# Rotary embedding on half the head, f32: interleaving batches on partitions so that one shuffle spreads the tables

## The chip, the cores and the metric

One core of a Trainium2 chip. (The sets of runs below came from different chips; each set has the kernel before beside it.) The metric is the device time of one execution in microseconds (us). A time is a median over runs; runs of one kernel mostly agree within 0.3%, and all runs quoted here are fast (granted clock 1.00). Profiles give a span that is about 1.8 us shorter than the measured time of the same run.

## The reference

```
x: (16, 512, 16, 64) f32    cos, sin: (512, 32) f32
x1, x2 = x[..., :32], x[..., 32:]
first  = x1[..., :16] * cos[..., :16] - x1[..., 16:] * sin[..., :16]
second = x1[..., :16] * sin[..., :16] + x1[..., 16:] * cos[..., :16]
out = concatenate([first, second, x2])
```

x is 33.55 MB and out is 33.55 MB. Half of every head is only copied, so the kernel moves 67.1 MB and computes on half of what it loads. The tables depend on the sequence position alone, not on the batch.

## The kernel before

x is seen as 512 runs of 16 sequence positions, 64 KB each. A tile is 128 consecutive runs, one per partition, and there are four tiles and a ring of three buffers. A batch has 32 runs, so partition p needs table row p mod 32: the 32 rows are loaded onto partitions 0 to 31 and copied four times.

```
    xf = x.rearrange("b s h d -> (b s h d)").rearrange("(t p f) -> t p f", t=T, p=P)
    of = out.rearrange("b s h d -> (b s h d)").rearrange("(t p f) -> t p f", t=T, p=P)
    ...
    ring = const_pool.tile([P, NS, K, H, D], fp32)          # NS = 3, K = 16
    stage = const_pool.tile([PB, 2, K, HF], fp32)           # PB = 32
    table = const_pool.tile([P, 2, K, 2, Q], fp32)
    ...
    nc.gpsimd.dma_start(out=stage[:, 0]..., in_=cosf)
    nc.gpsimd.dma_start(out=stage[:, 1]..., in_=sinf)
    load(0, 0, K0); load(0, K0, K); load(1); load(2, 0, KC)  # K0 = 4, KC = 8, on nc.sync
    for r in range(REP):                                     # REP = 4
        nc.vector.tensor_copy(out=table[r * PB : (r + 1) * PB]..., in_=stage...)
    ...                     # rotate: two multiplies, a subtract, an add on VectorE
    rotate(0, 0, K0); rotate(0, K0, (K0 + K) // 2); rotate(0, (K0 + K) // 2, K)
    store(0); load(2, KC, K); load(3)
    for t in range(1, T):
        rotate(t, 0, KC); rotate(t, KC, K); store(t)
```

All loads of x and all stores go through one queue (q1 on the page, 67.11 MB), and they follow each other in the order of issue: tile 0, tile 1, half of tile 2, store 0, the other half of tile 2, tile 3, and the stores of tiles 1, 2 and 3.

Of the kernel before, what the change touches and what calls it, by code (L numbers as in the profile page):

```python
# [1 line left out]

# [4 lines left out]


@with_exitstack
def kernel(  # L10
    ctx: ExitStack,
    tc: tile.TileContext,
    x: bass.AP,
    cos: bass.AP,
    sin: bass.AP,
    out: bass.AP,
):
    nc = tc.nc
    fp32 = mybir.dt.float32
    P = 128  # L20
    B, S, H, D = x.shape
    Q = D // 4
    HF = D // 2



    K = 16
    T = B * S // (P * K)
    PB = S // K
    REP = P // PB  # L30
    R = H * D
    NS = 3
    KC = K // 2
    K0 = K // 4

    xf = x.rearrange("b s h d -> (b s h d)").rearrange("(t p f) -> t p f", t=T, p=P)
    of = out.rearrange("b s h d -> (b s h d)").rearrange("(t p f) -> t p f", t=T, p=P)
    cosf = cos.rearrange("(p k) j -> p (k j)", k=K)
    sinf = sin.rearrange("(p k) j -> p (k j)", k=K)

    const_pool = ctx.enter_context(tc.tile_pool(name="const", bufs=1))
    b_pool = ctx.enter_context(tc.tile_pool(name="bp", bufs=1, space=bass.MemoryType.PSUM))


    ring = const_pool.tile([P, NS, K, H, D], fp32)
    stage = const_pool.tile([PB, 2, K, HF], fp32)
    table = const_pool.tile([P, 2, K, 2, Q], fp32)

    def rows(t, lo, hi):
        return ring[:, t % NS, lo:hi].rearrange("p k h d -> p (k h d)")  # L50

    def load(t, lo=0, hi=K):
        nc.sync.dma_start(out=rows(t, lo, hi), in_=xf[t, :, lo * R : hi * R])  # L53

    def store(t, lo=0, hi=K):
        nc.sync.dma_start(out=of[t, :, lo * R : hi * R], in_=rows(t, lo, hi))

    nc.gpsimd.dma_start(out=stage[:, 0].rearrange("p k j -> p (k j)"), in_=cosf)  # L58
    nc.gpsimd.dma_start(out=stage[:, 1].rearrange("p k j -> p (k j)"), in_=sinf)  # L59
    load(0, 0, K0)  # L60
    load(0, K0, K)
    load(1)
    load(2, 0, KC)


    for r in range(REP):
        nc.vector.tensor_copy(  # L67
            out=table[r * PB : (r + 1) * PB].rearrange("p t k c j -> p (t k) c j"),
            in_=stage.rearrange("p t k j -> p (t k) j")[:, :, 0:Q]
            .unsqueeze(2)  # L70
            .to_broadcast((PB, 2 * K, 2, Q)),
        )
    C = table[:, 0].rearrange("p k c j -> p k (c j)")
    Sn = table[:, 1].rearrange("p k c j -> p k (c j)")

    def rotate(t, lo, hi):
        n = hi - lo
        x1 = ring[:, t % NS, lo:hi, :, 0:HF]
        c = C[:, lo:hi].unsqueeze(2).to_broadcast((P, n, H, HF))
        s = Sn[:, lo:hi].unsqueeze(2).to_broadcast((P, n, H, HF))  # L80
        b_full = b_pool.tile([P, KC, H, HF], fp32, name="b_t")
        b_t = b_full[:, 0:n]
        nc.vector.tensor_mul(out=b_t, in0=x1, in1=s)  # L83
        nc.vector.tensor_mul(out=x1, in0=x1, in1=c)  # L84
        nc.vector.tensor_sub(  # L85
            out=x1[:, :, :, 0:Q], in0=x1[:, :, :, 0:Q], in1=b_t[:, :, :, Q:HF]
        )
        nc.vector.tensor_add(  # L88
            out=x1[:, :, :, Q:HF], in0=x1[:, :, :, Q:HF], in1=b_t[:, :, :, 0:Q]
        )  # L90

    rotate(0, 0, K0)
    rotate(0, K0, (K0 + K) // 2)
    rotate(0, (K0 + K) // 2, K)
    store(0)
    load(2, KC, K)
    load(3)
    for t in range(1, T):
        rotate(t, 0, KC)
        rotate(t, KC, K)  # L100
        store(t)


# [1 line left out]
_INS = ['x', 'cos', 'sin']  # L105
_OUTS = [((16, 512, 16, 64), 'float32')]


# [23 lines left out]
```

## Time and profile before

| | before |
|---|---|
| time, median | 161.8 us |
| span of the profile | 160.1 us |
| DMA queue of x and out, share of 16 engines | 97.8% |
| VectorE busy | 110.0 us (69%) |
| first multiply starts | 11.94 us |

The DMA queue lines of the page (queue, kind: packets, MB, share of the time of 16 engines):

```profile
q1 hardware_dynamic: 1440, 67.11, 97.8%
q0 software_dynamic: 64, 0.13, 0.2%
```

The table by stage (stretch in us, its length, busy us and instructions of VectorE and GpSimd, clock, DMA share, GB/s):

```profile
10.00:50.00 40.00, 34.92 (x17) 0.00 (x0) 1.00 1.00 434
50.00:100.00 50.00, 47.55 (x15) 0.00 (x0) 1.00 1.00 430
100.00:156.00 56.00, 26.68 (x8) 0.00 (x0) 1.00 1.02 440
```

The kernel is bound by its transfers: from 10 to 156 us the 16 engines are busy all the time (DMA share 1.00 to 1.02) at 430 to 440 GB/s. VectorE, busy for 69% of the span, has slack.

The start of the timeline (start us, us, engine, line, operation; in brackets the idle time before and what ended it; DVE is VectorE, POOL is GpSimd, SPq is SyncE, which issues the transfers of x and out):

```profile
0.74 1.88 SPq L53 DMA_DIRECT2D ring<-in_x_dram  x4
1.25 0.63 POOL L58 DMA_DIRECT2D stage<-in_cos_dram  x1 [0.81 <-PEq L127]
...
9.13 2.77 DVE L67 COPY table<-stage 32x1024 f32<-32x1024 f32 x4 [9.13 <-DMA stage<-in_sin_dram]
11.94 2.30 DVE L83 TENSOR_TENSOR b_t<-ring,table 128x2048 f32<-128x2048 f32 x1
...
23.66 3.37 DVE L83 TENSOR_TENSOR b_t<-ring,table 128x3072 f32<-128x3072 f32 x1 [4.71 <-DMA ring<-in_x_dram]
```

The chain of waits, its transfers only (start us, us, what):

```profile
0.74 0.38 SPq L53
...
1.17 22.39 DMA ring<-in_x_dram
...
44.14 28.18 DMA out_dram<-ring
72.34 28.75 DMA ring<-in_x_dram
```

The ends of these pieces are landings: the rest of tile 0 landed at 23.56 us, store 0 at 72.32 us, tile 3 at 101.09 us.

### The profile page before, as it was taken

Reading aid. Unit: us, or ns where it says so; the run is one execution under the profiler, and the core shown is the slowest. Engines: PE = TensorE matmul, PEld = TensorE weight load, DVE = VectorE, ACT = ScalarE, POOL = GpSimd, SP = SyncE. Lnnn points to the kernel's source line nnn. Section 1 sums busy time; section 2 is a strip of 40 time slices with the busy share of each in tenths; the row PEclk is TensorE's granted clock in tenths of the full one; section 3 lists DMA queues with packets and bytes.
Section 4 is the critical chain, followed back from the end, with each engine's and each line's share of the span. In section 5 each row is a group of like instructions: output and inputs, shape, how many; then the busy total and the mean of one; then the engine's idle time right before and its main releaser. Section 6 shows DMA issues by size and latency. Waiting matters only on the chain.

```text
span 160.1 us, 109 instructions
## 1 busy us (share of the span) xinstructions
DVE 110.0 (69%) x40; POOL 1.3 (1%) x6
## 2 busy tenths in 40 slices
DVE  0069709999999999999999994799999900000000
POOL 3000000000000000000000000000000000000000
DMA  6999999699699799899996996996996996996991
GB/s 197 385 504 454 393 459 524 262 524 491 295 401 581 328 524 409 377 393 418 483 540 295 491 524 262 524 524 262 524 524 262 524 524 262 524 491 295 524 459 66
DMA packets 1504, 67.24 MB, mean 420 GB/s; under 512 B 192, under 2 KB 192, under 8 KB 224
## 3 DMA queue, kind: packets, MB, share of 16 engines
q1 hardware_dynamic: 1440, 67.11, 97.8%
q0 software_dynamic: 64, 0.13, 0.2%
HBM read 33.69 MB, written 33.55 MB: 420 GB/s over the span
## 4 chain that ended last, share of the span: by engine, by line
DMA 50%; DVE 28%; DVEq 1%; issue 0%; SPq 0%
DMA ring<-in_x_dram 32%; DMA out_dram<-ring 18%; DVE b_t L83 10%; DVE ring L84 10%; DVE ring L85 5%; DVE ring L88 3%; DVEq L127 1%; SPq L53 0%; DVEq L83 0%
## 5 line engine op out<-in xcount | busy, mean ns | idle before, releaser
L83 DVE TENSOR_TENSOR b_t<-ring,table 128x4096 f32<-128x4096 f32 (+2 forms) x9 | 35.6, 3959 | 8.2 <-DMA ring<-in_x_dram 8.0
L84 DVE TENSOR_TENSOR ring<-ring,table 128x4096 f32<-128x4096 f32 (+2 forms) x9 | 35.6, 3950 | 0.3
L85 DVE TENSOR_TENSOR ring<-ring,b_t 128x2048 f32<-128x2048 f32 (+2 forms) x9 | 18.4, 2049 | 0.3
L88 DVE TENSOR_TENSOR ring<-ring,b_t 128x2048 f32<-128x2048 f32 (+2 forms) x9 | 18.4, 2042 | 0.0
L67 DVE COPY table<-stage 32x1024 f32<-32x1024 f32 x4 | 2.7, 684 | 9.2 <-DMA stage<-in_sin_dram 9.1
L58 POOL DMA_DIRECT2D stage<-in_cos_dram x1 | 0.6, 631 | 0.8 <-PEq L127 0.8
L59 POOL DMA_DIRECT2D stage<-in_sin_dram x1 | 0.5, 498 | 0.0
L116 POOL MEMSET const-bfloat16-1.0<- 128x1 bf16 x1 | 0.1, 102 | 0.0
L116 POOL MEMSET const-float32-0.0<- 128x1 f32 x1 | 0.1, 99 | 0.2 <-issue 0.2
L116 POOL MEMSET const-float32-1.0<- 128x1 f32 x1 | 0.1, 99 | 0.0
L116 POOL MEMSET const-uint8-127<- 128x1 uint8 x1 | 0.1, 99 | 0.0
## 6 DMA issues: line engine op xcount, KB each, us to landing
ring<-in_x_dram SPq DMA_DIRECT2D x2, 4096.0 KB, 43.9
ring<-in_x_dram SPq DMA_DIRECT2D x1, 6144.0 KB, 22.4
ring<-in_x_dram SPq DMA_DIRECT2D x1, 2048.0 KB, 8.5
stage<-in_cos_dram POOLq DMA_DIRECT2D x1, 64.0 KB, 6.0
stage<-in_sin_dram POOLq DMA_DIRECT2D x1, 64.0 KB, 7.2
out_dram<-ring SPq DMA_DIRECT2D x4, 36.4
ring<-in_x_dram SPq DMA_DIRECT2D x2, 35.0
```

The source lines that it names most:

```text
L58: nc.gpsimd.dma_start(out=stage[:, 0].rearrange("p k j -> p (k j)"), in_=cosf)
L59: nc.gpsimd.dma_start(out=stage[:, 1].rearrange("p k j -> p (k j)"), in_=sinf)
L67: nc.vector.tensor_copy(out=table[r * PB : (r + 1) * PB].rearrange("p t k c j -> p (t k) c j"), in_=stage.rearrange("p t k j -> p (t k) j" ...
L83: nc.vector.tensor_mul(out=b_t, in0=x1, in1=s)
L84: nc.vector.tensor_mul(out=x1, in0=x1, in1=c)
L85: nc.vector.tensor_sub(out=x1[:, :, :, 0:Q], in0=x1[:, :, :, 0:Q], in1=b_t[:, :, :, Q:HF])
L88: nc.vector.tensor_add(out=x1[:, :, :, Q:HF], in0=x1[:, :, :, Q:HF], in1=b_t[:, :, :, 0:Q])
L116: nc = _bacc.Bacc("TRN2", target_bir_lowering=False, num_devices=1)
L127: with _tile.TileContext(nc) as tc:
```

## The change

The intent is to spread the tables by one VectorE instruction for all 128 partitions instead of four for 32. The shuffle of the edit is given one mask with 32 entries, p // 4 * 4, for the 128 partitions, and the four partitions that need one table row are made neighbours: partition 4j+b takes run j of batch b, the table rows land on every fourth partition, and one shuffle copies each to the next three. The part of the stage that is read is first set to zero on all 128 partitions, and the table loads wait for that.

```diff
-    xf = x.rearrange("b s h d -> (b s h d)").rearrange("(t p f) -> t p f", t=T, p=P)
-    of = out.rearrange("b s h d -> (b s h d)").rearrange("(t p f) -> t p f", t=T, p=P)
+    xf = x.rearrange("(t b) (j k) h d -> t j b (k h d)", t=T, k=K)
+    of = out.rearrange("(t b) (j k) h d -> t j b (k h d)", t=T, k=K)
 ...
-    stage = const_pool.tile([PB, 2, K, HF], fp32)
+    stage = const_pool.tile([P, 2, K, HF], fp32)
 ...
-    nc.gpsimd.dma_start(out=stage[:, 0].rearrange("p k j -> p (k j)"), in_=cosf)
-    nc.gpsimd.dma_start(out=stage[:, 1].rearrange("p k j -> p (k j)"), in_=sinf)
+    nc.vector.memset(stage[:, :, :, 0:Q], 0.0)
+    first = stage.rearrange("(j b) t k i -> j b t (k i)", b=REP)
+    nc.gpsimd.dma_start(out=first[:, 0, 0], in_=cosf)
+    nc.gpsimd.dma_start(out=first[:, 0, 1], in_=sinf)
 ...
-    for r in range(REP):
-        nc.vector.tensor_copy(...)
+    nc.vector.stream_shuffle(out=table..., in_=stage...,
+        mask=[p // REP * REP for p in range(32)])
```

The transfers of x and out now have three dimensions on the HBM side (32 runs, 4 batches 2 MB apart, the row) instead of two.

More of the change, by code (lines that the diff above doesn't have):

```diff
@@ L52, in load @@
     def load(t, lo=0, hi=K):
-        nc.sync.dma_start(out=rows(t, lo, hi), in_=xf[t, :, lo * R : hi * R])
+        nc.sync.dma_start(out=rows(t, lo, hi), in_=xf[t, :, :, lo * R : hi * R])
     def store(t, lo=0, hi=K):
-        nc.sync.dma_start(out=of[t, :, lo * R : hi * R], in_=rows(t, lo, hi))
-    nc.gpsimd.dma_start(out=stage[:, 0].rearrange("p k j -> p (k j)"), in_=cosf)
-    nc.gpsimd.dma_start(out=stage[:, 1].rearrange("p k j -> p (k j)"), in_=sinf)
+        nc.sync.dma_start(out=of[t, :, :, lo * R : hi * R], in_=rows(t, lo, hi))
+    nc.vector.memset(stage[:, :, :, 0:Q], 0.0)
+    first = stage.rearrange("(j b) t k i -> j b t (k i)", b=REP)
+    nc.gpsimd.dma_start(out=first[:, 0, 0], in_=cosf)
+    nc.gpsimd.dma_start(out=first[:, 0, 1], in_=sinf)
     load(0, 0, K0)
@@ L63 @@
     load(2, 0, KC)
-    for r in range(REP):
-        nc.vector.tensor_copy(
-            out=table[r * PB : (r + 1) * PB].rearrange("p t k c j -> p (t k) c j"),
-            in_=stage.rearrange("p t k j -> p (t k) j")[:, :, 0:Q]
-            .unsqueeze(2)
-            .to_broadcast((PB, 2 * K, 2, Q)),
-        )
+    nc.vector.stream_shuffle(
+        out=table.rearrange("p t k c j -> p (t k) c j"),
+        in_=stage.rearrange("p t k j -> p (t k) j")[:, :, 0:Q]
+        .unsqueeze(2)
+        .to_broadcast((P, 2 * K, 2, Q)),
+        mask=[p // REP * REP for p in range(32)],
+    )
     C = table[:, 0].rearrange("p k c j -> p k (c j)")
```

## The prediction

> **What bounds it now.** The 16 DMA engines. The page's queue line gives the x/out queue 97.8% of 16 engines' span, and a table by stage reads 434, 430 and 440 GB/s in 10-50, 50-100 and 100-156 us, at a DMA share of 1.00 to 1.02: every engine always has a packet.[...] 67.11 MB at 434 GB/s is 154.6 us; about 2 us of start, 1 us lost in 2-10 us (373 GB/s) and 3 us of end complete the span of 160.1. VectorE is busy for 110.0 us (69%) and idles 32 us at the end.
>
> **What the change does.**
> 1. Table spread: four 32x1024 copies (684 ns each, 2.77 us in the timeline) become one 128x1024 shuffle.[...] Estimate 1.2-1.4 us, saving about 1.4.
> 2. Added: a 128x512 memset, an estimated 0.4-0.7 us, and the table loads (issued at 1.25 us) now wait for it: about 0.5 us later. Table rows also land on every fourth partition[...]. I expect landing at 9.5-11.5 us instead of 9.1; the first multiply starts between 11 and 13 us (11.94 before). Nearly a wash.
> 3. Moved: partition 4j+b takes run j of batch b. Bytes, row lengths (16 to 64 KB) and transfers stay; four neighbouring partitions are now 2 MB apart in HBM instead of adjacent, and the HBM side has one more dimension. Packets should still be one per row, on all 16 engines. Issue may get slower (four loads take 1.88 us now), perhaps by 0.1-0.3 us each; only the first counts.
>
> **On the critical path.** Almost nothing. VectorE ends the first quarter tile at 18.95 us and then waits 4.71 us for the second load, so a table earlier or later by up to 4.7 us changes no store. Even that load isn't binding: the store of tile 0 is issued at 44.1 us while about 20 MB of loads keep the engines busy to about 50 us. The chain of waits puts 28% on VectorE, but the saturated stages show that work to be covered. So I expect 0 to +0.3 us from a later first transfer, and no gain from the shuffle.
>
> **Predicted time**: 161.9 us; 161.4 to 163.0 should hold it 8 times in 10. Faster by over 2%: 0.01; within 2%: 0.94; slower by over 2%: 0.05.
>
> **What would show the steps right.** One shuffle of 1.1-1.5 us in the groups view; the wait for the table ends at 9.5-11.5 us; the wait before the second multiply takes up what the table stage lost or won; it ends at 23.3-24.3 us; main-stage rate 430-440 GB/s; 1440 packets on the x/out queue; VectorE busy about 109 us.
>
> **What would make it wrong.** (a) HBM disliking the new order[...]. [...]I don't expect it; it would show as a rate below 425 GB/s. (b) Transfers divided over fewer or unevenly loaded engines[...]; the DMA share would fall[...]. (c) A table landing later than about 16 us. (d) A start later by more than 0.3 us.

Passages of the recorded text that rested on rules not shown by any trace of this case are cut; the places are marked. The forecast's sum is the 161.8 us measured before plus 0 to 0.3 us for a later first transfer, which came to 161.9 us. The 0.4 to 0.7 us for the memset and the 0.1 to 0.3 us for a slower issue are estimates, with no derivation.

## The result, and the profile after

The changed kernel took 163.44 us median (162.95 to 164.49, 6 runs) against 161.80 us (161.75 to 162.16, 6 runs): a ratio of 1.0101, 95% interval 1.0068 to 1.0134. (Ratios divide the mean time of one kernel's fast runs by that of the other's of the same rounds, so they are not quite the ratio of the medians.) It is clearly slower by about 1%, 163.44 us where 161.9 were predicted. The outputs are right.

DMA queue lines of the page, after:

```profile
q1 hardware_dynamic: 1440, 67.11, 97.3%
q0 software_dynamic: 64, 0.13, 0.2%
```

The table by stage, after:

```profile
10.00:50.00 40.00, 33.58 (x15) 0.00 (x0) 1.00 1.00 427
50.00:100.00 50.00, 47.28 (x15) 0.00 (x0) 1.00 1.01 430
100.00:156.00 56.00, 26.68 (x8) 0.00 (x0) 1.00 0.99 431
```

These stages count a packet's bytes where it starts, and 16 packets of 64 KB are 1 MB, so differences of some GB/s over 50 us are not meaningful. They show no general slowdown.

The start of the timeline, after:

```profile
0.73 2.65 SPq L54 DMA_DIRECT2D ring<-in_x_dram  x4
0.92 0.48 DVE L59 MEMSET stage<- 128x512 f32 x1 [0.92 <-PEq L120]
1.71 0.65 POOL L61 DMA_DIRECT2D stage<-in_cos_dram  x1 [1.26 <-DVE stage L59]
...
8.95 0.01 DVE L70 LOAD_MASK_SELECT table<-stage  x1 [7.55 <-DMA stage<-in_sin_dram]
8.98 1.29 DVE L70 STREAM_SHUFFLE table<-stage 128x1024 f32<-128x1024 f32 x1
10.30 2.30 DVE L87 TENSOR_TENSOR b_t<-ring,table 128x2048 f32<-128x2048 f32 x1
...
23.39 3.37 DVE L87 TENSOR_TENSOR b_t<-ring,table 128x3072 f32<-128x3072 f32 x1 [6.08 <-DMA ring<-in_x_dram]
```

VectorE did what was intended. The shuffle took 1.29 us instead of the 2.77 of the four copies, and the first multiply starts 1.64 us earlier. The four first issues take 2.65 us instead of 1.88.

The chain of waits, its transfers only, after:

```profile
0.73 0.67 SPq L54
...
1.46 21.84 DMA ring<-in_x_dram
...
43.88 29.38 DMA out_dram<-ring
73.27 29.00 DMA ring<-in_x_dram
```

This is where the time went. The rest of tile 0 landed at 23.30 us, 0.26 **earlier** than before. Store 0 landed at 73.26 us, 0.94 **later**. So 1.20 us were lost between these landings. VectorE is no part of it: its work on tile 0 ended, and store 0 was issued, earlier than before (43.88 against 44.14 us).

The packet records of the trace show the place. Nearly all packets run at one pace: 65,536 bytes in 2418 ns, 27.1 GB/s per engine. Each row of a transfer is one packet (128 packets of 16 KB, 128 of 48, 256 of 32 and 768 of 64 for the ten transfers of 128 rows; the other 160 of the page's 1440 have 4 bytes), which makes 8 per engine and transfer. (The records do not name the engine: the n-th packets are the n-th sixteen of a transfer in order of start.) Below is the mean duration, in ns, of the 16 engines' n-th packet: first for the first quarter of tile 0 (16 KB, full pace about 605 from the 64 KB packets, fastest seen 608), then for the first half of tile 2, the last load before store 0 (32 KB, full pace 1213).

```
              1st  2nd  3rd  4th  5th  6th  7th  8th
16 KB before 1211  650  614  621  628  775  659  896
16 KB after   908  640  629  626  658  633  622  638
32 KB before 1215 1217 1216 1216 1218 1218 1216 1272
32 KB after  1213 1213 1213 1219 1217 1213 1821 2035
```

Two things changed, with opposite signs. Before, the small packets were held up around 6 to 8 us, while the table rows landed; after, they are not. But after, the last two packets of the load ahead of store 0 take on average 1.5 and 1.7 times as long, and all sixteen of each are slow; before, they hardly are.

I call **loss** the time that packets took beyond 27.1 GB/s, summed over a stretch and divided by 16 engines. It does not count the time in which an engine moves packets of the table in between. Before: 1.27 us in the first 10 us, 0.11 us at the first change from loads to stores. After: 0.52 and 1.47 us. The first x packet also starts later, at 2.19 instead of 1.75 us. Together: +0.44 - 0.75 + 1.36 = +1.05 us, and the landing of the first half of tile 2, as a mean over the engines, moved by as much, from 52.38 to 53.43 us. By the last store the mean is 0.96 us later; its slowest engine is a further 0.22 us behind, which makes the 1.2 us between the two spans. (The profiled run, 163.01 us, was one of the faster ones of this kernel; the medians are 1.6 us apart.)

### The profile page after: what moved, and what is told of

It reads as the page before. It is cut to its first block, busy times and chain, and to the rows that moved or that the text cites. A ratio compares the mean times of both kernels' runs of the same rounds, so it can differ in the third digit from the quotient of the medians.

```text
span 161.2 us, 108 instructions
## 1 busy us (share of the span) xinstructions
DVE 109.1 (68%) x39; POOL 1.4 (1%) x6
## 3 DMA queue, kind: packets, MB, share of 16 engines
q1 hardware_dynamic: 1440, 67.11, 97.3%
## 4 chain that ended last, share of the span: by engine, by line
DMA 50%; DVE 28%; DVEq 1%; SPq 0%; issue 0%
DMA ring<-in_x_dram 32%; DMA out_dram<-ring 18%; DVE b_t L87 10%; DVE ring L88 10%; DVE ring L89 5%; DVE ring L92 3%; DVEq L131 1%; SPq L54 0%; DVEq L87 0%
## 5 line engine op out<-in xcount | busy, mean ns | idle before, releaser
L70 DVE STREAM_SHUFFLE table<-stage 128x1024 f32<-128x1024 f32 x1 | 1.3, 1287 | 0.0
L59 DVE MEMSET stage<- 128x512 f32 x1 | 0.5, 485 | 0.9 <-PEq L120 0.9
```

Of the source, the lines that this page charges most:

```text
L59: nc.vector.memset(stage[:, :, :, 0:Q], 0.0)
L70: nc.vector.stream_shuffle(out=table.rearrange("p t k c j -> p (t k) c j"), in_=stage.rearrange("p t k j -> p (t k) j")[:, :, 0:Q] .unsque ...
```

## The experiments

The questions: which part of the change does it (table, issue, row order in HBM), and are the gain at the start and the loss at the change of direction independent, or does one follow from the other? The first theory was that the transfers themselves are slower in the new order. The rivals were the table loads, and the longer issue. The table has all runs that keep the order of transfers and, but for the change's own, the row order in HBM: the median time, and readings of each run's profile, all in us. A **hold-up** is a stretch before the first change in which packets of x are lengthened; "loss later" is what fell between 10 and 46 us.

```
                  time    first   loss before  loss     loss at   tile 0 landed
                          packet  10 us        later    change    (mean engine)
before           161.80   1.75    1.27         -        0.11      23.30
before_again     161.96   1.74    1.09         -        0.24      23.16
before_no_table  162.02   1.75    0.69         -        1.25      22.25
table_only       162.65   1.74    0.70         -        1.34      22.62
long_issue       162.29   2.09    0.96         -        0.47      23.42
long_2           162.40   2.08    0.82         -        0.67      23.27
table_long       162.85   2.08    0.67         -        1.17      22.91
layout_only      162.57   2.21    0.85         -        0.72      23.39
layout_2         162.51   2.19    0.81         -        0.77      23.32
after_low32      162.54   2.20    0.91         -        0.52      23.47
after_dummy      162.78   2.19    0.69         0.44     0.46      23.90
after_late_dummy 163.11   2.18    0.49         0.55     0.42      22.89
after            163.44   2.19    0.52         -        1.47      22.94
again            163.19   2.18    0.56         -        1.49      22.92
```

("-" stands for about 0.1 us or less.) The kernel before, rerun beside each set, was 161.95 to 162.08 us.

### The changed kernel again

No edit.

> The changed kernel itself once more, for a second profile and its scatter. The first profile lost its time in one place: 32 KB packets of the first half load of tile 2, which took 1.8 to 2.4 us each instead of 1.21 in the stage around 47 to 52 us. If that is a property of the change, the same stretch shows it again and the median stays at 163.2 to 163.8; if it was an accident of one profile, the slow packets lie elsewhere or are gone.

163.19 us (162.96 to 163.96), ratio 1.0078 (1.0059 to 1.0097). The same two packets are slow (1828 and 2062 ns), loss 1.49 us. So it belongs to the change. The profiled run was the slowest of its set, 163.96 us, and in it one engine finished the last store 1.3 us behind the mean; in the first profile (163.01 us) the slowest was 0.22 us further behind than in the kernel before.

### Row order alone

```diff
 (kernel before; wrong values)
-    xf = ...("(t p f) -> t p f", t=T, p=P)          # and of
+    xf = x.rearrange("(t b) (j k) h d -> t j b (k h d)", t=T, k=K)   # and of
```

> The kernel before with the new row order for x and out alone (partition 4j+b), the table still made by four copies; wrong values on purpose. Theory order (the transfers themselves are slower, through order in HBM or through the third dimension): 163.2 to 163.8 us, the whole loss. Theory table (memset, later table loads, shuffle): 161.8.

162.57 us, ratio 1.0028 (1.0014 to 1.0041). Neither theory's number: the row order, with the longer issue that comes with it (0.66 us for the first one, 0.38 before), carries about half the loss of time.

### Table alone

```diff
 (changed kernel; wrong values)
-    xf = x.rearrange("(t b) (j k) h d -> t j b (k h d)", t=T, k=K)   # and of
+    xf = ...("(t p f) -> t p f", t=T, p=P)          # and of
```

> The changed kernel with the row order of before, so that only the table is made the new way; wrong values on purpose. Theory order: 161.6 to 161.9 us, no loss. Theory table: 163.2 to 163.8.

162.65 us, ratio 1.0038 (1.0024 to 1.0051). The new table is not harmless, although not one address of x or out has changed. Its chain of waits, transfers only:

```profile
1.16 21.67 DMA ring<-in_x_dram
...
43.41 29.50 DMA out_dram<-ring
72.93 28.87 DMA ring<-in_x_dram
```

Tile 0 landed at 22.83 us, 0.73 us earlier than before, and store 0 at 72.91 us, 0.59 us later: a gain turned into a loss. So the slow packets do not need the new row order in HBM, and it showed the two effects side by side.

### Longer issue alone

The edit, to the kernel before: one line in the launch turns a setting of the program's builder off. No line of the kernel itself changes. What the setting does is told here by the trace alone: with it off, the first issue took 0.56 us, against 0.38 in the kernel before and 0.67 in the changed kernel.

> The kernel before, addresses unchanged, [...]all transfers are issued as the three-dimensional ones of the changed kernel are (0.54 to 0.67 us instead of 0.33 to 0.50). Theory issue: it carries the loss, 163.2 to 163.8 us. Theory HBM order: only the first issue counts, 161.9 to 162.2 us.

162.29 us, ratio 1.0012 (0.9997 to 1.0027); a repeat below gave 162.40 us, 1.0024 (1.0011 to 1.0037). So the issue itself carries 0.3 to 0.4 us, far from the whole loss; the first of the two runs is not clear of noise. Its first packet is 0.34 us later than that of before, not 0.44 as in the changed kernel: the setting brings back most of the delay, not all.

The sum of the parts: row order with its issue 0.54 and table 0.62 us over the 162.03 us of the kernel before in the same set, 1.16 together; the changed kernel was 1.16 us over it in that set. So the parts add up.

### The kernel before again

No edit.

> The kernel before once more, for a second profile of it. In its first profile the packets lost 1.27 us per engine against full pace before 10 us (while the table rows landed) and 0.11 us at the first change from loads to stores (load half 2 to store 0). In the six profiles so far the two go against each other: (1.27, 0.11), (0.96, 0.48), (0.85, 0.73), (0.70, 1.35), (0.56, 1.50), (0.52, 1.47). Expect near (1.2, 0.2) again if both belong to the kernel; anything like (1.2, 1.3) would break the pattern.

161.96 us, loss 1.09 us at the start and 0.24 at the change. The pattern held, so the low loss at the change is a property of the kernel before and not of one profile.

### Changed kernel, table rows on partitions 0 to 31

```diff
 (changed kernel; wrong values)
-    first = stage.rearrange("(j b) t k i -> j b t (k i)", b=REP)
-    nc.gpsimd.dma_start(out=first[:, 0, 0], in_=cosf)            # and sin
+    first = stage.rearrange("p t k i -> p t (k i)")
+    nc.gpsimd.dma_start(out=first[0:PB, 0], in_=cosf)            # and sin
```

> The changed kernel, but the table rows land on partitions 0 to 31 as before (wrong values on purpose); memset, shuffle and row order stay. Theory trade (where the rows land sets both the loss at the start and, inversely, the loss at the first change from loads to stores): start loss back to 0.85 or more, loss at the change down to 0.3 to 0.8, time down to 162.4 to 162.7, the value of the run with the row order alone. Theory memset or shuffle: the time stays at 163.1 to 163.5.

162.54 us, ratio 1.0035 (1.0019 to 1.0051), as the trade theory had it. The chain, transfers only:

```profile
1.45 22.33 DMA ring<-in_x_dram
...
44.36 28.33 DMA out_dram<-ring
72.71 28.83 DMA ring<-in_x_dram
```

Tile 0 landed at 23.78 us, 0.48 later than in the changed kernel, and store 0 at 72.69 us, 0.57 **earlier**. Memset, shuffle and row order were all still there. Where the table rows land is what matters: on 32 adjacent partitions they hold up the x packets (the eighth took 857 ns on average), on every fourth partition they hardly do (638 in the changed kernel).

### Kernel before without table loads

```diff
 (kernel before; wrong values)
-    nc.gpsimd.dma_start(out=stage[:, 0]..., in_=cosf)            # and sin
+    nc.vector.memset(stage[:, :, :, 0:Q], 1.0)
```

> The kernel before with no table loads at all (the stage is set to a constant; wrong values on purpose), so nothing disturbs the first x packets. Theory trade: start loss 0.5 us or less, and yet the loss at the first change from loads to stores rises to 1.3 us or more, so that the kernel does not get faster, 161.9 to 162.8. Theory plain cost (the table loads cost 0.75 us at the start and nothing else follows from them): 161.0 to 161.2 us, with 0.1 at the change.

162.02 us, ratio 0.9999 (0.9986 to 1.0012). Here the traffic of the tables is gone, and the kernel is not faster. The chain, transfers only:

```profile
1.16 21.27 DMA ring<-in_x_dram
...
43.01 29.55 DMA out_dram<-ring
72.58 28.80 DMA ring<-in_x_dram
```

Tile 0 landed 1.13 us earlier than in the kernel before (22.43 against 23.56), and store 0 0.24 us later. The seventh and eighth packets ahead of the change took 1932 and 1726 ns. In the table above, tile 0 landed 0.37 us earlier than with the tables on every fourth partition (22.25 against 22.62, table_only), at the same loss before 10 us. Most of that is the time in which the engines moved the tables themselves: with the tables the packet records leave 0.28 us per engine between one packet of x and the next, and nothing without them. (The loss before 10 us, 0.69, is more than the 0.5 expected: it is the first packet of each engine, 1204 ns, which is slow in the kernels before and after as well, 1211 and 908 ns where full pace is 605.)

### Changed kernel, tile 2 loaded whole

```diff
 (changed kernel)
-    load(2, 0, KC)
+    load(2)
 ...
-    load(2, KC, K)
```

> The changed kernel with tile 2 loaded whole ahead of store 0 instead of in halves around it, so that the first change from loads to stores comes one half tile later, behind 64 KB rows, and one change of direction is the same. If the loss belongs to a change that finds the store issued only about 5 us before (half load), it falls to the 0.0 to 0.3 us of the second change, and the time to 161.7 to 162.2. If it belongs to the first change as such, it stays at 1.3 to 1.5 and the time at 163.1 to 163.5.

172.19 us, ratio 1.0625 (1.0608 to 1.0641). The time says nothing of the question. In this program store 1 (issued at 70.65 us) comes ahead of the load of tile 3 (82.53 us), tile 3 landed late (VectorE waited 23.86 us for it), and the engines ran dry, as this line of its table by stage shows:

```profile
140.00:149.00 9.00, 8.19 (x3) 0.00 (x0) 1.00 0.00 0
```

But the packets do say something. The first change now comes at about 62 us, behind rows of 64 KB, with store 0 issued at 43.75 us, long before. Now it is the last 64 KB packet of all 16 engines that is slow, 1.38 to 1.47 times full pace, about 1.0 us; the packets around 47 to 51 us are within about 3% of full pace. So in this run the loss goes with the change of direction, not with a point in time, nor with half loads, nor with a store issued just before it. It falls on about the last 64 KB of each engine's loads.

### Useless loads at the start

```diff
 (changed kernel, correct)
+    spare = const_pool.tile([PB, 2, K, HF], fp32)
+    nc.gpsimd.dma_start(out=spare[:, 0]..., in_=cosf)
+    nc.gpsimd.dma_start(out=spare[:, 1]..., in_=sinf)
     load(0, 0, K0)
```

> The changed kernel, correct, with extra work: cos and sin are loaded a second time, onto partitions 0 to 31 of a spare tile that nobody reads, at the start. Theory trade (packets that are held up early save more at the first change to stores): start loss up from 0.52 to 0.9 or more, loss at the change down from 1.47 to 0.6 or less, and the kernel gets faster by doing more, 162.3 to 162.8 us. Theory of independent costs: start loss up by 0.3 or more, change unchanged at 1.3 to 1.5, time 163.5 to 164.2.

162.78 us, ratio 1.0045 (1.0031 to 1.0059): more traffic, and faster than the changed kernel (163.19 and 163.44). The hold-up came later than I had expected, 0.44 us of it at 12 us, so that the loss before 10 us rose only to 0.69; the loss at the change fell to 0.46.

### Useless loads late

```diff
 (changed kernel, correct; after the second third of tile 0)
+    nc.vector.tensor_copy(out=spare[:, 0, 0], in_=ring[0:PB, 0, K0, 0, 0:HF])   # and spare[:, 1, 0]
+    nc.gpsimd.dma_start(out=spare[:, 0]..., in_=cosf)                           # and sin
     rotate(0, (K0 + K) // 2, K)
```

> The changed kernel, correct, with the same two useless loads, but issued when the second third of tile 0 is rotated, at about 34 us, that is well after the start and 13 us before the first change to stores. If what counts is that the engines were held up at some time before the change, the loss at the change falls to 0.6 or less and the time to 162.3 to 162.9. If only the very start sets it, the change keeps 1.3 to 1.5 us and the time is 163.2 to 163.9.

163.11 us, ratio 1.0066 (1.0052 to 1.0080). The time lies between the two forecasts (162.3 to 162.9 and 163.2 to 163.9) and is not clear of the changed kernel's own (ratio 1.0059 to 1.0097 in the run above), but the packets decide: most of the hold-up of 0.55 us fell at 39.5 to 43 us, and the loss at the change dropped to 0.42. The chain:

```profile
1.45 21.81 DMA ring<-in_x_dram
...
43.99 28.87 DMA out_dram<-ring
72.88 28.90 DMA ring<-in_x_dram
```

From the landing of tile 0 to that of store 0 it took 49.60 us, against 49.96 in the changed kernel, although 0.55 us of hold-up now lie in this stretch. So a hold-up shortly before the change acts too, not only one at the start.

### Everything but the row order

The edit, to the kernel of table alone (wrong values): the same line in the launch as in longer issue alone. The first issue took 0.56 us, 0.37 in table alone.

> The new table with the old row order[...]: everything of the changed kernel except the order of rows in HBM and the third dimension as such (wrong values on purpose). If the row order in HBM costs nothing, this equals the changed kernel: 162.9 to 163.5 us, first packet as late as in the changed kernel, loss at the first change 1.3 to 1.5. If the order has its own price, 162.6 to 162.8.

162.85 us, ratio 1.0043 (1.0030 to 1.0055), in the gap between the two expectations. It lacks only the row order and the third dimension, and is 0.3 to 0.6 us short of the changed kernel.

### Third dimension without the 2 MB spacing

```diff
 (row order alone; wrong values)
-    x.rearrange("(t b) (j k) h d -> t j b (k h d)", t=T, k=K)        # and out
+    x.rearrange("b s h d -> (b s h d)").rearrange("(j t b f) -> t j b f", t=T, b=4, f=K * R)   # and out
```

> The kernel before with three-dimensional transfers in which, unlike the changed kernel's, four neighbouring partitions still read adjacent 64 KB runs of HBM (partition 4j+b takes run 16j+4t+b; wrong values on purpose; the groups of four are then 1 MB apart, not 256 KB). The row order alone measured 162.57 us, the long issue alone 162.29. If the 0.28 us between them is the third dimension (a first issue of 0.66 instead of 0.56 us), this is 162.5 to 162.7; if it is four rows 2 MB apart in HBM, 162.2 to 162.4.

163.71 us, ratio 1.0103 (1.0089 to 1.0117). Neither. With groups of four runs 1 MB apart, this order has a price of its own: 0.45 us lost outside the start and the changes to stores, part of it around 69 to 74 us, where stores turn to loads, and 0.58 us at the second change to stores, where the row order of the change loses 0.01 to 0.07. So it can't split the third dimension from the spacing, and that question stays open. It shows that the order of rows in HBM mattered by about 1 us here (163.71 us, against 162.51 for the row order of the change).

### Row order alone and longer issue alone, on one chip

No new edit: both runs again, on the chip of the run above.

> The row order alone once more, on the chip of the run above: 162.4 to 162.7 us, start loss 0.8 to 0.9, loss at the first change 0.5 to 0.8.

> The long issue alone once more, on the chip of the two runs above: 162.2 to 162.4 us, start loss 0.9 to 1.0, loss at the first change 0.4 to 0.6. A difference to the row order alone of less than 0.1 us would mean that there is nothing left to split.

162.51 us, ratio 1.0032 (1.0018 to 1.0046), for the row order alone, and 162.40 us, ratio 1.0024 (1.0011 to 1.0037), for the longer issue alone. On one chip the difference is 0.11 us, within the scatter of long_2 (162.18 to 162.57). Most of what the row order costs is its issue, and since the setting does not delay the first packet quite as much (2.08 against 2.19 us), even these 0.11 us may be issue. What else it costs, 0.1 to 0.3 us there and 0.3 to 0.6 beside the new table, is not split further.

## Why the prediction was right or wrong

**Right.** What bounds the kernel, and what VectorE does. The shuffle took 1.29 us (1.2 to 1.4 predicted, an estimate): 1287 ns in the trace, against 1220 ns for the subtract of the same 128x1024 in the profile before. The memset took 0.485 us (0.4 to 0.7). The wait before the second multiply took up what the table stage won: 4.71 + 1.64 - 0.27 = 6.08 us, as measured. Packets stayed at 1440, the DMA share at 97%, VectorE busy 109.1 us. Of the four dangers only (d), a later start, came true.

**Wrong: "a table earlier or later by up to 4.7 us changes no store", hence "0 to +0.3 us from a later first transfer".** The step treated the table as a matter of when it lands for VectorE. But its loads take time of the engines that move x: with them the records leave 0.28 us per engine between packets of x, without them nothing. Landing on 32 adjacent partitions, they lengthened the x packets by 0.4 to 0.6 us in all at the start (1.27 and 1.09 us lost before 10 us, 0.69 without table loads); landing on every fourth partition, by next to nothing (0.70 with the new table alone). (They also landed earlier, at 8.95 us and not in the predicted 9.5 to 11.5, so the first multiply started at 10.30, not at 11 to 13.) That alone would have been a gain: with the new table alone, tile 0 landed 0.68 us earlier in the mean. It was more than taken back at the first change from loads to stores, where the loss went from 0.11 to 1.47 us (1.34 with the new table alone). The prediction has no term for that change at all; the experiment with the table alone puts the net at +0.62 us.

**Mis-sized: the later first transfer.** Issues got slower by 0.2 to 0.3 us each as predicted (0.54 to 0.67 us instead of 0.33 to 0.50), but the first packet came 0.44 us later, and with its share of the loss at the change the row order cost 0.5 to 0.6 us in place of 0 to 0.3.

**What is shown, and what is only argued.** Shown, with one profile of each run: in the table, a kernel that lost 0.8 us or more before the first change loses 0.1 to 0.8 us there, and one that lost 0.7 or less loses 1.2 to 1.5; putting the table rows back on partitions 0 to 31, or adding useless loads early or late, lowers that loss; taking the table loads away raises it. Only argued: why. One more reading fits: for the load of tile 1, ahead of the change, the landing follows the end of the last packet's record by 0.47 us on average over the engines in the kernels of the table that were held up early (0.56 after the late hold-up), and by 0.39 to 0.41 us in those that were not. So a hold-up may leave the engines with more data under way, and that may cover the turn to stores. No run separates this from other explanations. One of them the packet records speak against: that it depends on how far apart the engines are when they reach the change. The first packets of the load ahead of it start within 0.50 us of each other in the kernel before (0.11 us lost), 0.36 without table loads (1.25 lost), 0.28 in long_2 (0.67 lost) and 0.72 in the changed kernel (1.47 lost), in no order.

No version beat the kernel before. Hold-up and loss at the change add up to 1.3 to 1.6 us in the kernels that were held up, and to 1.8 to 2.1 in the others, and in time a hold-up was paid back in full (the kernel before against the one without table loads) or more (useless loads at the start). But no run shows that tuning it wins anything over the kernel before.

## What to carry to other kernels

Where the DMA engines are full from end to end, as here (97.8% of the span), judge a small side load by what it does to the packets of the large transfers, not by when it lands; and compare the landings of the large transfers one after another, for here an early gain was gone two landings later (changed kernel, means over the engines: tile 0 landed at 22.94 us instead of 23.30, the first half of tile 2 at 53.43 instead of 52.38). Removing a disturbance that is visible in the profile is no gain until the time says so: here taking all table loads away did not move it (ratio 0.9999, 0.9986 to 1.0012). Instructions saved on an engine with slack were worth nothing here (the first multiply started 1.64 us earlier, and the wait before the second grew from 4.71 to 6.08 us), and with the longer issue of the three-dimensional transfers (0.67 us for the first one instead of 0.38) the first packet came 0.44 us later.

## What was measured of the transfers

- Two loads of 64 KB onto partitions 0 to 31 lengthened 16 KB packets of a concurrent transfer in some rounds: 775 and 896 ns in the mean for the sixth and eighth of each engine, against 614 to 659 for the third to fifth and the seventh (before). Onto every fourth partition, with the same bytes, the packets took 622 to 658 from the third on (after). Why the place makes this difference, no run shows.
- At the first turn of the queue from loads to stores, the last 64 KB or so of each engine ran in the mean at 0.6 to 0.7 of full pace in some kernels, 1.2 to 1.5 us lost (after: 1213 ns at full pace, 1821 and 2035 measured), and near full pace (0.1 to 0.2 us lost in the kernel before) or in between (0.4 to 0.8) in others; those that were held up earlier lost less. A second turn cost 0.0 to 0.3 us, with one row order (third_dim) 0.6.
- From the end of the first issue to the first packet it was 0.63 us before (1.12 to 1.75) and 0.79 after (1.40 to 2.19). An issue of the three-dimensional transfers took 0.54 to 0.67 us, one of the two-dimensional 0.33 to 0.50, and the first packet came 0.44 us later.
- With four neighbouring rows 2 MB apart the steady stages kept full pace (64 KB in 2418 ns, after); groups of four adjacent rows, the groups 1 MB apart, took 1.2 us longer than that order (163.71 against 162.51 us, third_dim and layout_2).
